# Layer 1's feed-forward block by seven block products in place of eight

## The chip, the cores and the metric

The kernel runs on 1 core of one Trainium2 chip. The metric is device time in microseconds (us), the median of the runs shown. TensorE (PE) does the matmuls, VectorE (DVE) and ScalarE (ACT) elementwise work, GpSimd (POOL) more of it, SyncE (SP) issues all the DMAs.

## What is computed

Two transformer layers over 1024 latent tokens (and 256 context tokens, which only layer 0 carries to its end), model width 1024, FFN width 2816. The change touches only the second layer's SwiGLU block and what leads into it and out of it:

```python
def swiglu(h, w_in, w_out):
    g, u = jnp.split(h @ w_in, 2, axis=-1)
    return (jax.nn.silu(g) * u) @ w_out
...
        x = x + g1 * rms_norm(y, norm_g[l, 1])
        h = rms_norm(x, norm_g[l, 2]) * (1.0 + sc2) + sh2
        x = x + g2 * rms_norm(swiglu(h, ffn_w_in[l], ffn_w_out[l]), norm_g[l, 3])
```

## The kernel before, in words

Activations are held transposed: features on the 128 partitions, tokens along the row. Tokens come in chunks, "a" (0 to 511) and "b" (512 to 1023) in layer 1. A matmul takes a 128x128 weight block and 128x512 activations. Operands are split in two parts, hi and lo (`split`, L396: ACT casts hi, DVE subtracts to get lo), and each product is three matmuls, hi by hi, hi by lo and lo by hi (`mm3`, L404). So 16 weight blocks of a hidden row block (8 for gate, 8 for up) on one chunk are 48 matmuls.

`OutFFN` (L1543) is the output projection and the FFN of one layer. `run` (L1680) first does the projection of chunk a (`p1`) and of b (`p2`), 192 matmuls each. `after` (L1589) follows for each chunk: the residual (`g_residual`, L577), the store of x to DRAM (`X1`), and the second norm (`g_modnorm`, L555), each with a `rstd` (L495: eight one-column matmuls with `ones`, a chain of twelve small POOL instructions) and a `bcast` (L526: four transposes into a bank that DVE then reads). The FFN then goes over NJ = 22 hidden row blocks j. For each j and chunk, `gu` (L1630) does gate and up (48 matmuls) and the activation, and `down` (L1648) multiplies it by the eight 128-column blocks of the down weights (24 matmuls) into eight banks. DVE adds each of those banks to a sum in SBUF. So a j takes 144 matmuls, and the FFN of layer 1 takes 22 x 144 = 3168.

```python
        for f in range(KT):
            ps = pr.b()[:, :n]
...
            pr.mm3(ps, [(wh[:, s], wl[:, s], ah, al)])
            if j == 0:
                pr.nc.scalar.copy(y[f], ps)
            else:
                pr.add(y[f], y[f], ps)
```

The order of the work is not the order of the code. `Recorder` (L48) records every instruction with a cost and its dependencies; `issue` (L160) then plays a list schedule, earliest recorded first among those that are ready and have room in the pools, and emits each engine's instructions in that order. The chip keeps this order on each engine. All instructions therefore carry the line L260 in the profile. Pools: 44 tiles T of 128x1024, 13 tiles U of 128x512, 8 banks b. Names such as T_5897 in the orders below are tiles of those pools.

Of the kernel before, what the change touches and what calls it, by code (L numbers as in the profile page):

```python
# [25 lines left out]
HID = 2816  # L26
NJ = HID // P
# [23 lines left out]
class Recorder:  # L51
# [211 lines left out]
class FM:  # L263
# [7 lines left out]
    def __getitem__(self, kt):  # L271
        o = (kt % self.per) * self.n
        return self.tiles[kt // self.per][:, o:o + self.n]


class Prog:
# [1266 lines left out]
class OutFFN:  # L1543
# [78 lines left out]
    def begin(self):  # L1622
        for k in "gu":
            self.fetch(k, 0)
        for k in "gu":
            self.cv(k, 0)
        for k in "ogu":
            self.fetch(k, k != "o")
# [82 lines left out]
                pr.long(self.finish(c))  # L1711


def program(ctx, nc, tc, d, out):
    nc = Recorder(nc)
    pr = Prog(ctx, nc, tc, d, out)
    pr.setup()
    src0 = {"a": d["xT"][:, 0:512], "b": d["xT"][:, 512:1024], "c": d["ctxT"]}
    h0, h1 = {}, {}
    OT0, OT1 = pr.dram([D, 2, TOK]), pr.dram([D, 2, TOK])  # L1720
    X2 = pr.dram([D, TOK], F32)

# [40 lines left out]
    nc.issue()  # L1763
# [87 lines left out]
```

## Time and profile before

| what | value |
| --- | --- |
| median of 3 runs | 3366.03 us (3363.17 to 3368.88) |
| the profiled execution's own time | 3368.35 us |
| its span, first to last instruction | 3366.3 us |
| PE busy | 3230.5 us (96%) |
| PEld (weight loads) busy | 2677.7 us (80%) |
| DVE, ACT, POOL busy | 2117.3, 1403.2, 617.2 us (63%, 42%, 18%) |
| DMA | 318.20 MB, mean 95 GB/s |

The profiled execution is one more run than the three; it is 2.3 us above their median. Busy shares are averages over stages that have different limits. Layer 1's FFN takes the last fifth of the span, from about 2612 us on.

### The profile page before, as it was taken

How to read it: one execution, taken by the hardware profiler on the slowest of the kernel's cores; microseconds unless marked ns; L12 is line 12 of the kernel's file. 1: busy time of each engine (PE TensorE's matmuls, PEld its weight loads, DVE VectorE, ACT ScalarE, POOL GpSimd, SP SyncE). 2: the span in 40 equal slices, each digit the busy share in tenths (PEclk: the TensorE clock that was granted, in tenths of full speed). 3: DMA queues.
4: the chain of work that ended last, by engine and by line, in shares of the span. 5: the costliest groups of instructions: out<-in, count | busy, mean ns of one | idle time of the engine just before them, and what ended most of it. 6: DMA issues, size and time to landing. Idle time of an engine off the chain costs nothing.

```text
span 3366.3 us, 45397 instructions
## 1 busy us (share of the span) xinstructions
PE 3230.5 (96%) x16916; PEld 2677.7 (80%) x16916; DVE 2117.3 (63%) x4129; ACT 1403.2 (42%) x3208; POOL 617.2 (18%) x943
## 2 busy tenths in 40 slices
PE   7988999999999999999999998999999999999997
PEld 5877778887888888888877896667777788888886
DVE  5569888846444444444478638989985544445445
ACT  3369877854411111111134316778984411111111
POOL 2311100015100000000044716760004200000003
PEclk8999999999999999999999999999999999999998
DMA  6263655344111111111133235432144111111111
GB/s 239 76 221 104 207 160 156 111 161 163 44 38 38 38 38 38 38 38 38 63 115 118 100 117 132 131 110 85 59 170 149 63 57 39 55 51 43 57 57 63
DMA packets 129324, 318.20 MB, mean 95 GB/s; under 512 B 11408, under 2 KB 32592, under 8 KB 129104
## 3 DMA queue, kind: packets, MB, share of 16 engines
q1 hardware_dynamic: 129104, 315.31, 28.8%
q8 instruction: 133, 2.18, 0.3%
q14 instruction: 87, 0.71, 0.1%
HBM read 243.63 MB, written 71.63 MB: 94 GB/s over the span
## 4 chain that ended last, share of the span: by engine, by line
PE 78%; DVE 9%; ACT 4%; POOL 3%; issue 3%; DMA 2%; SPq 0%; POOLq 0%; ACTq 0%; DVEq 0%
PE b L260 78%; DVE T L260 4%; DVE U L260 3%; DVE S L260 3%; ACT T L260 3%; POOL S L260 2%; ACT U L260 2%; POOL U L260 1%; DMA T<-in_ada_w_dram 1%; DMA scr<-T 1%; SPq L260 0%; DMA T<-in_ctxT_dram 0%; POOL T L260 0%; ACT S L260 0%; POOLq L1846 0%
## 5 line engine op out<-in xcount | busy, mean ns | idle before, releaser
L260 PE MATMUL b<-T,T 128*128 128x512 f32 (+5 forms) x9958 | 2172.2, 368 | 33.4 <-ACT T L260 12.8
L260 PEld LDWEIGHTS b<-T,T 128*128 128x128 f32 (+2 forms) x9958 | 1711.7, 190 | 353.4 <-ACT T L260 33.9
L260 PE MATMUL b<-U,T 128*128 128x512 f32 (+2 forms) x3808 | 937.0, 379 | 10.1 <-DVE U L260 3.8
L260 PEld LDWEIGHTS b<-U,T 128*128 128x128 f32 x3808 | 661.4, 189 | 123.0 <-ACT U L260 5.5
L260 DVE TENSOR_TENSOR U<-U,b 128x512 f32<-128x512 f32 (+3 forms) x214 | 134.0, 627 | 619.8 <-PE b L260 607.8
L260 POOL TENSOR_TENSOR U<-U,U 128x512 f32<-128x512 f32 (+1 forms) x130 | 174.9, 1349 | 1696.1 <-ACT U L260 1692.0
L260 DVE TENSOR_TENSOR T<-T,b 128x512 f32<-128x512 f32 (+1 forms) x840 | 482.0, 629 | 0.0
L260 DVE TENSOR_TENSOR T<-T,T 128x1024 fp32r<-128x1024 f32 (+4 forms) x274 | 314.9, 1163 | 232.0 <-PE b L260 173.1
L260 DVE TENSOR_REDUCE S<-b 128x1 f32<-128x512 f32 (+1 forms) x672 | 374.5, 569 | 62.1 <-PE b L260 57.4
L260 ACT ACTIVATE T<-b,S 128x512 f32<-128x512 f32 (+1 forms) x640 | 385.5, 609 | 47.9 <-DVE S L260 42.8
L260 ACT CAST T<-T 128x1024 fp32r<-128x1024 f32 (+3 forms) x202 | 206.1, 1024 | 344.9 <-PE b L260 296.8
L260 DVE TENSOR_TENSOR U<-b,U 128x512 fp32r<-128x512 f32 (+3 forms) x528 | 335.8, 647 | 20.7 <-ACT U L260 16.8
L260 ACT ACTIVATE U<-b 128x256 f32<-128x256 f32 (+1 forms) x148 | 81.3, 552 | 621.6 <-PE b L260 621.3
L260 PE MATMUL b<-ident,T 128*128 128x128 f32 x1968 | 316.7, 277 | 24.6 <-ACT T L260 14.1
L260 ACT CAST U<-b 128x512 fp32r<-128x512 f32 (+3 forms) x528 | 291.1, 565 | 86.1 <-PE b L260 82.6
L260 PEld LDWEIGHTS b<-ident,T 128*128 128x128 f32 x1968 | 238.4, 141 | 89.0 <-ACT T L260 32.0
L260 ACT CAST U<-U 128x512 fp32r<-128x512 f32 (+1 forms) x110 | 63.3, 576 | 305.0 <-DVE U L260 301.0
L260 DVE TENSOR_TENSOR U<-U,U 128x512 fp32r<-128x512 f32 (+4 forms) x167 | 118.9, 712 | 41.1 <-POOL U L260 29.8
L260 ACT ACTIVATE U<-T 128x512 f32<-128x512 f32 (+1 forms) x174 | 96.2, 577 | 96.4 <-DVE T L260 90.3
L260 ACT ACTIVATION_READ_ACCUMULATOR T<-b,S 128x1 f32 x640 | 132.8, 207 | 0.0
L260 ACT CAST T<-U 128x512 fp32r<-128x512 f32 (+3 forms) x122 | 69.4, 572 | 130.9 <-DVE U L260 113.1
L260 POOL TENSOR_TENSOR T<-U,T 128x512 fp32r<-128x512 f32 (+1 forms) x40 | 48.1, 1202 | 386.3 <-ACT T L260 371.3
(71 smaller groups left out, 1519.4 us busy)
## 6 DMA issues: line engine op xcount, KB each, us to landing
scr<-T SPq DMA_DIRECT2D x114, 512.0 KB
T<-in_ada_w_dram SPq DMA_DIRECT2D x96, 512.0 KB
T<-in_ffn_in_dram SPq DMA_DIRECT2D x88, 512.0 KB
T<-scr SPq DMA_DIRECT2D x82, 512.0 KB
T<-scr SPq DMA_DIRECT2D x88, 256.0 KB
T<-in_ffn_out_dram SPq DMA_DIRECT2D x44, 512.0 KB
T<-in_w_out_dram SPq DMA_DIRECT2D x32, 512.0 KB
T<-scr SPq DMA_DIRECT2D x72, 128.0 KB
```

The costliest lines, as they stand in the source:

```text
L260: f(*args, **kw)
```

## The change

Take gate and up of a row block as one product: the weights are a 2x2 block matrix (gate and up by the two halves of the 1024 input features), the activations another (the two feature halves by chunks a and b). Plain multiplication takes eight block products. Winograd's form of Strassen's scheme takes seven, with sums and differences of weight blocks and of activation blocks formed beforehand, and sums of the products afterwards. A block product of gate and up is 4 x 3 = 12 matmuls, so a row block takes 84 in place of 96.

- Activations (`after`): seven sets of four split tiles: B11 and B21 from chunk a alone; B22, T1, T2, T3 and T4 from b and differences of a and b. They occupy 28 of the 44 T tiles.
- `early`: for the first 8 row blocks, the two products that need chunk a alone, with gate of chunk a kept in DRAM (`EA`). `run` does these 8 blocks while b's sets are made.
- `tile`: for each row block the other products (five for the first 8, seven for the other 14), in two banks, with the sums done by accumulation in the bank, by DVE and by POOL. `prep` forms the weight sums on POOL and splits them. The last product (T4) of a row block comes after the next one has begun. The result goes to DRAM (`ACT`).
- `down_all`: after all 22 row blocks, the down projection, also by seven products, for hidden halves and output halves: 7 x 11 steps of 12 matmuls that accumulate in PSUM over 11 row blocks. Each step loads 128x512 weight blocks (nine per t over the seven products) and 128x512 activation blocks (four per t) from DRAM, 256 KB each, forms sums on POOL and DVE, and splits both operands.

Matmuls: 22 x 84 + 77 x 12 = 2772 in place of 3168. The diff, cut to its core:

```diff
+class WinoFFN(OutFFN):
+    EARLY = 8
+    HALF = NJ // 2
...
+    def put_set(self, name, k, x):
+        pr = self.pr
+        t = pr.T(F32R)
+        hi, lo = t[:, 0:512], t[:, 512:1024]
+        pr.split(x, hi, lo)
+        self.sets.setdefault(name, {})[k] = (hi, lo)
+        if len(self.sets[name]) == 4:
+            self.ready.add(name)
+    def after(self, c):
...
+        if c == "a":
+            for kt in range(KT):
+                norm(kt)
+                self.put_set("B11" if kt < 4 else "B21", kt % 4, y[kt])
+                if kt % 2:
+                    yield 3.0
+            return
+        a = self.hf["a"]
+        for k in range(4):
+            norm(k)
+            norm(k + 4)
+            self.put_set("B22", k, y[k + 4])
+            pr.sub(a[k], y[k], a[k])
+            yield 2.6
+            self.put_set("T1", k, a[k])
+            pr.tt(y[k], y[k + 4], y[k], ALU.subtract, eng=nc.gpsimd)
+            pr.sub(a[k], y[k + 4], a[k])
+            self.put_set("T2", k, a[k])
+            yield 2.4
+            pr.tt(a[k + 4], a[k + 4], a[k], ALU.subtract, eng=nc.gpsimd)
+            self.put_set("T3", k, y[k])
+            self.put_set("T4", k, a[k + 4])
+            yield 2.4
+        self.hf.clear()
+    def prod(self, ps, name, w, o, first):
+        pr = self.pr
+        (wh, oh), (wl, ol) = w
+        x = self.sets[name]
+        for k in range(4):
+            hi, lo = x[k]
+            h, q = wh[:, oh + o + k * P:oh + o + k * P + P], wl[:, ol + o + k * P:ol + o + k * P + P]
+            pr.mm(ps, h, hi, first and k == 0, False)
+            pr.mm(ps, h, lo, False, False)
+            pr.mm(ps, q, hi, False, k == 3)
+        pr.tick(2.7)
+    def early(self, j):
+        pr, nc = self.pr, self.pr.nc
+        if j + 2 < self.EARLY:
+            self.fetch("g", j + 2)
+        if j + 1 < self.EARLY:
+            self.gsplit(j + 1)
+        w = self.conv.pop(("g", j))
+        x, z = pr.b(), pr.b()
+        e = pr.T()
+        self.prod(x, "B11", w, 0, True)
+        nc.scalar.copy(e[:, 0:512], x)
+        pr.until(lambda: "B21" in self.ready)
+        self.prod(z, "B21", w, 512, True)
+        pr.add(e[:, 512:1024], e[:, 0:512], z)
+        nc.scalar.activation(e[:, 512:1024], e[:, 512:1024], AF.Silu)
+        pr.load(self.EA[j * P:(j + 1) * P, :], e)
+    def prep(self, j):
...
+        g, u = self.raws.pop(("g", j)), self.raws.pop(("u", j))
+        gp = nc.gpsimd
+        s = pr.T()
+        pr.tt(s[:, 0:512], u[:, 0:512], u[:, 512:1024], ALU.add, eng=gp)
+        pr.tt(s[:, 512:1024], s[:, 0:512], g[:, 0:512], ALU.subtract, eng=gp)
+        hi, lo = pr.wsplit(s)
+        self.conv["s12", j] = ((hi, 0), (lo, 0))
+        pr.tt(u[:, 0:512], g[:, 0:512], u[:, 0:512], ALU.subtract, eng=gp)
+        t = pr.T(F32R)
+        pr.split(u[:, 512:1024], t[:, 0:512], t[:, 512:1024])
+        self.conv["u", j] = ((t, 0), (t, 512))
+        pr.tt(u[:, 512:1024], g[:, 512:1024], s[:, 512:1024], ALU.subtract, eng=gp)
+        hi, lo = pr.wsplit(u)
+        self.conv["s34", j] = ((hi, 0), (lo, 0))
+    def tile(self, j):
+        pr, nc = self.pr, self.pr.nc
+        late = j < self.EARLY
+        x, y = pr.b(), None
+        s12, s34, u = (self.conv.pop((k, j)) for k in ("s12", "s34", "u"))
+        act = pr.T()
+        if late:
+            e = self.raws.pop(("e", j))
+            s1, sa = e[:, 0:512], e[:, 512:1024]
+            self.last()
+        else:
+            g = self.conv.pop(("g", j))
+            s1, sa = pr.U(), pr.U()
+            self.prod(x, "B11", g, 0, True)
+            nc.scalar.copy(s1, x)
+            self.last()
+            z = pr.b()
+            self.prod(z, "B21", g, 512, True)
+            pr.add(sa, s1, z)
+            nc.scalar.activation(sa, sa, AF.Silu)
+        self.raw(j + 2)
+        y = pr.b()
+        self.prod(y, "T1", s12, 0, True)
+        s5 = pr.U()
+        nc.scalar.copy(s5, y)
+        self.prod(x, "T2", s12, 512, late)
+        sb = pr.U()
+        if late:
+            pr.add(sb, s1, x)
+            pr.tt(s5, s5, s1, ALU.add, eng=nc.gpsimd)
+        else:
+            nc.scalar.copy(sb, x)
+        self.prep(j + 1)
+        self.prod(y, "B22", s34, 512, False)
+        pr.add(sb, sb, y)
+        nc.scalar.activation(sb, sb, AF.Silu)
+        self.prod(x, "T3", s34, 0, False)
+        pr.add(s5, s5, x)
+        pr.mul(act[:, 512:1024], sb, s5)
+        def last():
+            self.prod(x, "T4", u, 0, False)
+            if late:
+                pr.add(s5, s1, x)
+                pr.mul(act[:, 0:512], sa, s5)
+            else:
+                pr.mul(act[:, 0:512], sa, x)
+            pr.later(lambda: pr.load(self.ACT[j * P:(j + 1) * P, :], act))
+            self.last = lambda: None
+        self.last = last
+    PRODS = ("P1", "P5", "P6", "P3", "P7", "P2", "P4")
+    def dload(self, k):
...
+        for a in {"P1": [(0, 0)], "P5": [(0, 1)], "P6": [(1, 1)], "P2": [(1, 0)]}.get(p, []):
+            act(*a)
+        for b in {"P1": [(0, 0)], "P5": [(1, 0), (1, 1)], "P6": [(0, 0)], "P3": [(0, 1)], "P7": [(0, 0), (1, 0)],
+                  "P2": [(0, 1)], "P4": [(1, 1)]}[p]:
+            w(*b)
+    def dprep(self, k):
...
+        if p == "P5":
+            if t % 2 == 0:
+                self.sw[t // 2] = pr.T()
+        s = self.sw[t // 2][:, (t % 2) * 512:(t % 2) * 512 + 512] if p in ("P5", "P6", "P3") else raw[0]
+        if p == "P1":
+            x = k1[:, lo]
+        elif p == "P5":
+            x = k1[:, lo]
+            pr.sub(x, k1[:, hi], x)
+            pr.tt(s, raw[0], raw[1], ALU.add, eng=gp)
+        elif p == "P6":
+            x = k1[:, lo]
+            pr.sub(x, k2[:, hi], x)
+            pr.tt(s, s, raw[0], ALU.subtract, eng=gp)
+        elif p == "P3":
+            x = k2[:, hi]
+            pr.tt(s, raw[0], s, ALU.subtract, eng=gp)
+        elif p == "P7":
+            x = k1[:, hi]
+            pr.sub(x, k2[:, hi], x)
+            pr.tt(s, raw[0], raw[1], ALU.subtract, eng=gp)
+        elif p == "P2":
+            x = k2[:, lo]
+        else:
+            x = k1[:, lo]
+            pr.sub(x, k2[:, lo], x)
+        ws, xs = pr.T(F32R), pr.T(F32R)
+        pr.split(s, ws[:, lo], ws[:, hi])
+        pr.split(x, xs[:, lo], xs[:, hi])
+        self.dop[k] = (ws, xs)
+    def down_all(self):
...
+        LOADS, PREPS = 4, 2
+        for k in range(LOADS):
+            self.dload(k)
+        for k in range(PREPS):
+            self.dprep(k)
+        for k in range(7 * H):
+            p, t = self.PRODS[k // H], k % H
+            self.dload(k + LOADS)
+            self.dprep(k + PREPS)
+            ws, xs = self.dop.pop(k)
+            kind = "x" if p in ("P1", "P6", "P7", "P4") else "y"
+            new = t == 0 and p in ("P1", "P5", "P2")
+            if new:
+                bank[kind] = [pr.b() for _ in range(4)]
+            for f in range(4):
+                wh, wl = (ws[:, o + f * P:o + f * P + P] for o in (0, 512))
+                ps = bank[kind][f]
+                pr.mm(ps, wh, xs[:, 0:512], new, False)
+                pr.mm(ps, wh, xs[:, 512:1024], False, False)
+                pr.mm(ps, wl, xs[:, 0:512], False, t == H - 1)
+            pr.tick(2.7)
...
+    def run(self, hook=None):
+        pr, first, rest = self.pr, self.first, self.rest
+        pr.drain_slow()
+        self.p1.run((len(first) * KT - 2, self.p2.start))
+        self.p2.run((KT - 3, self.begin))
+        pr.until(lambda: "B11" in self.ready)
+        for j in range(self.EARLY):
+            self.early(j)
+        self.raw(0)
+        self.raw(1)
+        self.prep(0)
+        pr.until(lambda: len(self.ready) == 7)
+        for j in range(NJ):
+            self.tile(j)
+        self.last()
+        while pr.bg:
+            pr.tick(0)
+        self.sets.clear()
+        self.down_all()
...
-    f1 = OutFFN(pr, 1, "ab", OT1, lambda c: X2[:, CHUNKS[c][0]:CHUNKS[c][0] + CHUNKS[c][1]], put3, None)
+    f1 = WinoFFN(pr, 1, "ab", OT1, lambda c: X2[:, CHUNKS[c][0]:CHUNKS[c][0] + CHUNKS[c][1]], put3, None)
```

The order of the two programs is the same, up to tile numbers, on PE, DVE, ACT and POOL until the end of layer 1's output projection. After it, three places matter.

DVE from the first instruction after chunk b's second `bcast` (the bank b_5901 before, b_5895 in the change). Before, it scales y into U (bank as a source) and subtracts hi:

```order
L260 SCALAR_TENSOR_TENSOR U_5910<-T_5785,der_80,b_5901 128x512
L260 SCALAR_TENSOR_TENSOR U_5911<-T_5785,der_80,b_5901 128x512
L260 SCALAR_TENSOR_TENSOR U_5912<-T_5786,der_80,b_5901 128x512
L260 SCALAR_TENSOR_TENSOR T_5906<-U_5910,mod_78,T_5902 128x512
L260 SCALAR_TENSOR_TENSOR T_5906<-U_5911,mod_78,T_5902 128x512
```

And in the change, where T_5896 is part of B22, T_5897 of T1, T_5899 of T3:

```order
L260 SCALAR_TENSOR_TENSOR T_5787<-T_5787,der_80,b_5895 128x512
L260 SCALAR_TENSOR_TENSOR T_5789<-T_5789,der_80,b_5895 128x512
L260 SCALAR_TENSOR_TENSOR T_5787<-T_5787,der_80,b_5895 128x512
L260 TENSOR_TENSOR T_5737<-T_5787,T_5737 128x512
L260 SCALAR_TENSOR_TENSOR T_5789<-T_5789,der_80,b_5895 128x512
L260 TENSOR_TENSOR T_5737<-T_5787,T_5737 128x512
L260 TENSOR_TENSOR T_5896<-T_5789,T_5896 128x512
L260 TENSOR_TENSOR T_5897<-T_5737,T_5897 128x512
L260 TENSOR_TENSOR T_5899<-T_5787,T_5899 128x512
```

Up to the split of the first row block's weight sums (T_5944 below) this goes on for 39 DVE instructions: 8 with a scalar and the bank, 3 additions from a bank, 27 with two SBUF sources of 128x512 and one of 128x1024. Beside them stand 11 POOL additions of 128x512, and from the transposes to the last early product 72 matmuls on PE.

PE at the end of the early products (bank b_5930) in the change, the first row block's T1 product in b_5953 and T2 in b_5948. T_5943 and T_5944 are the hi and lo of its weight sums:

```order
L260 MATMUL b_5930<-T_5835,T_5921 128x512 x2
L260 MATMUL b_5930<-T_5835,T_5922 128x512
L260 MATMUL b_5953<-T_5897,T_5943 128x512 x2
L260 MATMUL b_5948<-T_5898,T_5943 128x512 x2
L260 MATMUL b_5953<-T_5897,T_5944 128x512
L260 MATMUL b_5953<-T_5908,T_5943 128x512 x2
```

Before, the same place has the gate product of chunk b, as soon as each part of its activations (T_5902) is there:

```order
L260 MATMUL b_5901<-ident,S_5898 128x128 x4
L260 MATMUL b_5930<-U_5888,T_5868 128x512
L260 MATMUL b_5933<-T_5902,T_5844 128x512
L260 MATMUL b_5934<-T_5902,T_5846 128x512
L260 MATMUL b_5942<-T_5902,T_5870 128x512
```

Four matmuls of the first row block stand ahead of the one that needs T_5944; all others stand behind it.

DVE in the down projection. Before, between two row blocks, it adds banks to the sums in SBUF:

```order
L260 TENSOR_TENSOR U_6193<-U_6193,b_6192 128x512
L260 TENSOR_TENSOR T_5947<-T_5947,b_6196 128x512
L260 TENSOR_TENSOR T_5947<-T_5947,b_6197 128x512
L260 TENSOR_TENSOR U_6195<-U_6193,U_6194 128x512
L260 TENSOR_TENSOR T_5948<-T_5948,b_6198 128x512
```

In the change, at the start of the second product (P5), it makes the operands of the third (P6) and differences for the fifth (P7):

```order
L260 TENSOR_TENSOR T_6410<-T_6354,T_6410 128x512
L260 TENSOR_TENSOR T_6411<-T_6300,T_6411 128x512
L260 TENSOR_TENSOR T_6300<-T_6399,T_6300 128x512
L260 TENSOR_TENSOR T_6414<-T_6354,T_6414 128x512
L260 TENSOR_TENSOR T_6304<-T_6408,T_6304 128x512 x2
L260 TENSOR_TENSOR T_6415<-T_6302,T_6415 128x512
```

None of these has a bank as a source. From the first weight sum on POOL (T_6354) to the last operand of P6 stand 92 DVE instructions (89 of them with two SBUF sources), 42 POOL additions and, up to P6's last step, 400 matmuls.

## Rows read from the trace of the kernel before

**Rows 1.** Cores: span and mean granted clock.

```profile
core 0: 3366.3 us, clock 0.986
```

**Rows 2.** The page's chain of waits that ended last, shares by engine.

```profile
PE 78%; DVE 9%; ACT 4%; POOL 3%; issue 3%; DMA 2%; SPq 0%; POOLq 0%; ACTq 0%; DVEq 0%
```

**Rows 3.** Windows: stretch, length, busy us and count per engine, clock, DMA share, GB/s.

```profile
2750.00:2850.00 100.00, 100.00 (x443) 82.84 (x442) 48.81 (x71) 16.82 (x22) 0.00 (x0) 1.00 0.14 48
```

**Rows 4.** Timeline of SP in the FFN: start, length, transfer, count.

```profile
2696.56 1.41 SPq L260 DMA_DIRECT2D T<-in_ffn_in_dram  x2
...
2729.20 1.40 SPq L260 DMA_DIRECT2D T<-in_ffn_in_dram  x2
...
2761.84 1.40 SPq L260 DMA_DIRECT2D T<-in_ffn_in_dram  x2
```

**Rows 5.** Timeline of PE at the FFN's start, with idle before and releaser.

```profile
2596.61 19.56 PE L260 MATMUL b<-T,T 128*128 128x512 f32 x85
2616.01 0.94 PE L260 MATMUL b<-ones,U 128*128 128x1 f32 x8
2616.82 4.39 PE L260 MATMUL b<-T,T 128*128 128x512 f32 x18
2621.04 0.60 PE L260 MATMUL b<-ident,S 128*128 128x128 f32 x4
2621.39 13.89 PE L260 MATMUL b<-T,T 128*128 128x512 f32 x60
2636.56 1.42 PE L260 MATMUL b<-U,T 128*128 128x512 f32 x5 [1.27 <-ACT U L260]
2638.27 1.05 PE L260 MATMUL b<-ones,U 128*128 128x1 f32 x8 [0.29 <-POOL U L260]
2639.95 4.42 PE L260 MATMUL b<-U,T 128*128 128x512 f32 x18 [0.63 <-DVE U L260]
2644.64 0.65 PE L260 MATMUL b<-ident,S 128*128 128x128 f32 x4 [0.28 <-POOL S L260]
2645.05 0.48 PE L260 MATMUL b<-U,T 128*128 128x512 f32 x1
2646.96 22.37 PE L260 MATMUL b<-T,T 128*128 128x512 f32 x96 [1.43 <-ACT T L260]
```

**Rows 6.** Timeline of DVE, four places where POOL is idle.

```profile
2591.67 1.21 DVE L260 TENSOR_TENSOR T<-T,T 128x1024 fp32r<-128x1024 f32 x1
...
2623.00 1.29 DVE L260 TENSOR_TENSOR T<-T,T 128x512 f32<-128x512 f32 x2
...
2645.40 2.06 DVE L260 SCALAR_TENSOR_TENSOR U<-T,der,b 128x512 f32<-128x512 f32 x3 [3.40 <-PE b L260]
...
2704.58 3.67 DVE L260 TENSOR_TENSOR T<-T,b 128x512 f32<-128x512 f32 x6
```

**Rows 7.** Timelines of DVE and POOL: POOL by itself, then both at once.

```profile
2625.03 1.29 POOL L260 TENSOR_TENSOR U<-U,U 128x512 f32<-128x512 f32 x1 [4.30 <-ACT U L260]
...
2579.33 11.26 DVE L260 TENSOR_TENSOR T<-T,T 128x512 f32<-128x512 f32 x6
...
2574.53 17.20 POOL L260 TENSOR_TENSOR U<-U,U 128x512 f32<-128x512 f32 x9 [1.42 <-ACT U L260]
```

**Rows 8.** Windows ahead of the FFN, columns as in rows 3.

```profile
2580.00:2590.00 10.00, 5.90 (x29) 4.62 (x27) 10.00 (x6) 5.73 (x8) 9.84 (x6) 1.00 0.77 275
2590.00:2600.00 10.00, 10.00 (x43) 8.24 (x43) 5.83 (x9) 3.48 (x6) 6.31 (x14) 0.83 0.45 162
...
2585.00:2590.00 5.00, 0.90 (x7) 0.48 (x5) 5.00 (x3) 1.57 (x2) 4.92 (x4) 1.00 1.03 393
```

**Rows 9.** Timelines of PE and of SP at the end of the program.

```profile
3330.71 11.04 PE L260 MATMUL b<-U,T 128*128 128x512 f32 x48
...
3316.99 45.86 SPq L260 DMA_DIRECT2D out_dram<-T  x8
```

More of the change, by code (lines that the diff above doesn't have):

```diff
@@ L1711, in run, with __init__, norm, begin @@
                 pr.long(self.finish(c))
+class WinoFFN(OutFFN):
+    EARLY = 8
+    HALF = NJ // 2
+    def __init__(self, *args):
+        super().__init__(*args)
+        self.hf, self.sets, self.ready = {}, {}, set()
+        self.ACT = self.pr.dram([HID, 1024], F32)
+        self.EA = self.pr.dram([self.EARLY * P, 1024], F32)
+    def put_set(self, name, k, x):
[7 more added lines that the diff above has]
+    def after(self, c):
+        pr, l, nc = self.pr, self.l, self.pr.nc
+        n = CHUNKS[c][1]
+        y = self.y.pop(c)
+        acc2 = pr.accs()
+        yield from pr.g_residual(y, self.acc.pop(c), self.xsrc(c), pr.vec(pr.der[l], 1, c), acc2)
+        dst = self.view(self.X1, c)
+        for i, t in enumerate(y.tiles):
+            pr.load(dst[2 * i * P:2 * i * P + 2 * P, :].rearrange("(k p) n -> p k n", p=P),
+                    t.rearrange("p (k n) -> p k n", n=n))
+        cols = pr.rstd(acc2, n, D)
+        yield -RSW
+        rb = pr.bcast(cols)
+        A, Bv = pr.vec(pr.der[l], 2, c), pr.mvec(l, 3, c)
+        def norm(kt):
+            pr.stt(y[kt], y[kt], A(kt), rb[:, :n])
+            nc.scalar.activation(y[kt], y[kt], AF.Identity, bias=Bv(kt))
+        self.hf[c] = y
+        if c == "a":
[33 more added lines that the diff above has]
+        pr.tick(2.7)
+    def begin(self):
+        for j in range(2):
+            self.fetch("g", j)
+        self.gsplit(0)
+    def gsplit(self, j):
+        hi, lo = self.pr.wsplit(self.raws.pop(("g", j)))
+        self.conv["g", j] = ((hi, 0), (lo, 0))
+    def early(self, j):
[14 more added lines that the diff above has]
+        pr.load(self.EA[j * P:(j + 1) * P, :], e)
+    def raw(self, j):
+        if j < NJ:
+            for kind in "gu":
+                self.fetch(kind, j)
+            if j < self.EARLY:
+                e = self.raws["e", j] = self.pr.T()
+                self.pr.load(e, self.EA[j * P:(j + 1) * P, :])
+    def prep(self, j):
+        if j >= NJ:
+            return
+        pr, nc = self.pr, self.pr.nc
+        if j >= self.EARLY:
+            g = self.raws["g", j]
+            hi, lo = pr.wsplit(g)
+            self.conv["g", j] = ((hi, 0), (lo, 0))
+        g, u = self.raws.pop(("g", j)), self.raws.pop(("u", j))
[13 more added lines that the diff above has]
+    def tile(self, j):
+        pr, nc = self.pr, self.pr.nc
+        late = j < self.EARLY
[45 more added lines that the diff above has]
+        self.last = last
+    def last(self):
+        pass
+    PRODS = ("P1", "P5", "P6", "P3", "P7", "P2", "P4")
+    def dload(self, k):
+        if k >= 7 * self.HALF:
+            return
+        pr, H = self.pr, self.HALF
+        p, t = self.PRODS[k // H], k % H
+        def act(half, c):
+            j = t + half * H
+            if j not in self.at:
+                self.at[j] = pr.T()
+            pr.load(self.at[j][:, c * 512:(c + 1) * 512], self.ACT[j * P:(j + 1) * P, c * 512:(c + 1) * 512])
+        def w(r, s):
+            raw = pr.U()
+            j = t + s * H
+            pr.load(raw, pr.d["ffn_out"][self.l, j * P:(j + 1) * P, r * 512:(r + 1) * 512])
+            self.wr.setdefault(k, []).append(raw)
+        for a in {"P1": [(0, 0)], "P5": [(0, 1)], "P6": [(1, 1)], "P2": [(1, 0)]}.get(p, []):
[4 more added lines that the diff above has]
+    def dprep(self, k):
+        if k >= 7 * self.HALF:
+            return
+        pr, H = self.pr, self.HALF
+        gp = pr.nc.gpsimd
+        p, t = self.PRODS[k // H], k % H
+        raw = self.wr.pop(k)
+        k1, k2 = self.at.get(t), self.at.get(t + H)
+        lo, hi = slice(0, 512), slice(512, 1024)
+        if p == "P5":
[28 more added lines that the diff above has]
+        self.dop[k] = (ws, xs)
+        if p == "P4":
+            self.at.pop(t)
+            self.at.pop(t + H)
+    def down_all(self):
+        pr, nc, H = self.pr, self.pr.nc, self.HALF
+        self.at, self.wr, self.sw, self.dop = {}, {}, {}, {}
+        ya, yb = FMs(pr), FMs(pr)
+        self.yacc = {"a": ya, "b": yb}
+        bank = {}
+        LOADS, PREPS = 4, 2
[4 more added lines that the diff above has]
+        for k in range(7 * H):
+            p, t = self.PRODS[k // H], k % H
+            self.dload(k + LOADS)
[12 more added lines that the diff above has]
+            pr.tick(2.7)
+            if t < H - 1:
+                continue
+            if p == "P7":
+                self.acc["b"] = pr.accs(1 if self.next_norm else 2)
+            if p == "P4":
+                self.acc["a"] = pr.accs(1 if self.next_norm else 2)
+            for f in range(4):
+                ps = bank[kind][f]
+                if p == "P1":
+                    nc.scalar.copy(ya[f], ps)
+                elif p == "P5":
+                    nc.scalar.copy(yb[f + 4], ps)
+                elif p == "P6":
+                    nc.scalar.copy(yb[f], ps)
+                elif p == "P3":
+                    pr.add(yb[f], yb[f], ps)
+                elif p == "P7":
+                    pr.add(yb[f + 4], yb[f + 4], ps)
+                    pr.sq_add(self.acc["b"], yb[f], 512, 2 * f)
+                    pr.sq_add(self.acc["b"], yb[f + 4], 512, 2 * f + 1)
+                elif p == "P2":
+                    pr.add(ya[f], ya[f], ps)
+                else:
+                    nc.scalar.copy(ya[f + 4], ps)
+                    pr.sq_add(self.acc["a"], ya[f], 512, 2 * f)
+                    pr.sq_add(self.acc["a"], ya[f + 4], 512, 2 * f + 1)
+            if p == "P7":
+                pr.long(self.finish("b"))
+        pr.long(self.finish("a"))
+    def run(self, hook=None):
[17 more added lines that the diff above has]
+        self.down_all()
@@ L1714, in program, with __init__, __getitem__, tiles @@
+class FMs:
+    def __init__(self, pr):
+        self.pr, self.n, self.per, self.t = pr, 512, 2, {}
+    def __getitem__(self, kt):
+        i = kt // 2
+        if i not in self.t:
+            self.t[i] = self.pr.T()
+        return self.t[i][:, (kt % 2) * 512:(kt % 2) * 512 + 512]
+    @property
+    def tiles(self):
+        return [self.t[i] for i in range(4)]
 def program(ctx, nc, tc, d, out):
```

## The prediction

> **What bounds the kernel now.** I read first the cores: 3366.3 us at a mean clock of 0.986 [rows 1], so the throttle has little to give back. The chain of waits gives PE 78% and DVE 9% [rows 2]. A share is a mean over stages, so I went to the stage that changes. In a stretch of 100 us of layer 1's FFN, PE is busy for all 100.00 us at clock 1.00, DVE for 48.81, ACT for 16.82, POOL for nothing, and the DMAs take a share of 0.14 [rows 3]. That stage is bound by PE alone: a matmul fewer is time gained, at the price that PE pays there. SP issues each row block's loads every 32.64 us (2696.56, 2729.20, 2761.84) [rows 4]; a row block is 144 matmuls, so one costs 0.2267 us. Some matmul records are missing from a trace, so this is better than dividing by a count of records.
>
> The other engines matter once work is put on them. DVE alone takes 0.60 us from one 128x512 operation with two SBUF sources to the next (two in 1.29 us, the last one's tail included), 0.66 for one with a scalar and a bank, 0.61 for an addition from a bank, 1.21 for 128x1024 [rows 6]. A POOL addition alone takes 1.29 us. Where both engines had such work, DVE took 11.26 us for six (1.88 each) and POOL 17.20 us for nine (1.91 each) [rows 7]. 0.60 + 1.29 is 1.89: they took turns, and each waited out the other's whole instruction. So I add up the two engines' times wherever both are queued on two SBUF sources.
>
> **The change part by part.** The sum is made against the profiled execution, 3368.35 us by its own time, which is 2.3 above the median of 3366.03.
>
> *Matmuls.* 3168 - 2772 = 396 fewer, at 0.2267: **-89.8**.
>
> *Entry.* The old start of the FFN had five idle gaps on PE, 1.27 + 0.29 + 0.63 + 0.28 + 1.43 = 3.9 us, while chunk b's norm was made [rows 5]: -3.9. The norm's chain (squares on ACT, rstd on POOL, transposes, bcast) stays, and only PE's early products lie beside it. I step PE to the second `ones` at about 2636.0; POOL delivers at 2638.3, where the old `ones` began [rows 5], so PE waits 2.3, and about 1.3 more for the bcast: +3.6.
>
> Then the sets. Before, PE went on after 1.43 us, because the gate product takes chunk b's activations one by one. Now the first row block needs its weight sums' split T_5944, behind 39 DVE instructions: 8 x 0.66 + 3 x 0.61 + 27 x 0.60 + 1.21 = 24.5 us if POOL is out of the way [rows 6]. Eleven POOL additions stand beside them, 14.2 us alone [rows 7]. By strict turns that is 38.7; if POOL runs freely under the 11 instructions that read a bank (7.1 us, room for three), eight additions count, 8 x 1.29 = 10.3, and I get about **35**. That is my choice. No row shows a bank reader beside POOL. The Trainium skill, "SBUF — State Buffer", section "Who interferes with whom", says that only a DVE instruction with two SBUF inputs meets GpSimd's reads; by that the 35 holds, without it 38.7. DVE begins at 2645.40 [rows 6], so T_5944 is there at 2680.4. PE has 72 matmuls from the transposes at 2644.64 [rows 5], 16.3 us and 0.4 for the transposes, then four that do not need T_5944, 0.9: it stands at 2662.3. The wait is **+18** (24.5 gives 7.6, 38.7 gives 22). After a wait the clock is lower: behind a stretch of 5 us in which PE was busy for 0.90, the next 10 us ran at a granted 0.83, between 1.2 and 2.4 GHz [rows 8]; 0.17 x 10 is +1.7. Entry in all: -3.9 + 3.6 + 18 + 1.7 = **+19.4**.
>
> *Row blocks.* Eight late ones of 60 matmuls (13.6 us) and fourteen of 84 (19.0 us). I add DVE and POOL of a late one in turns to about 10 us of the 13.6 and take them as covered. What is left is banks that PE must accumulate into again as soon as DVE has read them: 0.25 us for each late block (nothing, to a whole bank addition of 0.61 [rows 6]) and 0.5 at the first block's second weight sums: +2.5, between 0 and 5. A late block moves about 2 MB (gate and up weights, EA, ACT), 154 GB/s where 393 has been seen [rows 8]: 0. At the last row block no next one covers T4: three two-source operations, one POOL addition in turn and one bank addition are 1.8 + 1.29 + 0.61 = 3.7 us, less the 7 matmuls between, 1.6: **+2.1**.
>
> *Down.* From P5's first weight sum to P6's last operand: 89 x 0.60 + 3 x 0.61 + 42 x 1.29 = 109.4 us in turns [rows 6, 7], against 400 x 0.2267 = 90.7 of PE and about 2.5 of work made ahead, 93.2. The bounds are 0 (the engines overlap after all) and 16.2. I take 12, nearer the upper end, since the only stretch in which both were queued shows turns, and some waiting for ACT's casts beside which POOL is free: **+12**, spread over P6. P6's operands are tiles that P5 frees, so DVE cannot run further ahead. P3, P7, P2 and P4 ask for less and cost 0 (P7 again has one sum on each engine per step, but its differences are made during P5). The 22 x 8 bank additions per chunk that DVE did are gone, which frees DVE and not PE: 0.
>
> *End.* The last matmul ends at 3341.75 and the program 24.5 us later, after the last norm and eight stores [rows 9]. The order after the last product is of the same kind: +0.3 for one more bank copy.
>
> **Sum:** -89.8 + 19.4 + 2.5 + 2.1 + 12 + 0.3 = -53.5. On the profiled execution 3314.9, on the median 3312.6: **3313**.
>
> **The rivals.**
> *R1, it is nearly all hidden.* DVE and POOL overlap better than rows 7 show, so the entry's wait is 7.6 and P6 does not stall: -89.8 + 9.0 + 2.1 + 2.0 = -76.7, **3289**. For it: one stretch alone shows turns, and a sum is less late if POOL is ahead. Against: that stretch is exact, 1.88 and 1.91 for 1.89.
>
> *R2, DVE and POOL set the pace for longer.* The entry is at its upper bound (+23.4), the late blocks at theirs (+4.9), P6 at 16.2, and each of the fourteen full blocks waits for one POOL addition more, 14 x 1.29 = 18.1: -89.8 + 23.4 + 4.9 + 2.1 + 16.2 + 18.1 = -25.1, **3341**. For it: POOL, idle before [rows 3], forms every weight sum. Against: a full block gives 19 us for much the same sums as a late one's 13.6.
>
> *R3, slower: the down phase waits for its transfers.* It loads 99 weight and 44 activation blocks of 256 KB, 143 in all, over 924 matmuls, 209.5 us. If they went one after another at the price of a lone store, 512 KB in 3.4 us (issued by 3362.85, program ended at 3366.3 [rows 9]), that is 486 us: 277 more than PE's, -53.5 + 277, about **3590**. It decides for slower from (209.5 + 53.5) / 143 = 1.84 us per transfer. Against: with several queued, the trace moves 393 GB/s [rows 8], 256 KB in 0.67 us; P5, the hungriest product, asks for three in 2.72 us, 289 GB/s, and loads stand four steps ahead, 10.9 us. The Trainium skill, "DMA: Bandwidth & Descriptors", section "Anatomy of one DMA", speaks against this change: for its GpSimd path it fits a fixed 2.0 us per DMA plus bytes over 436 GB/s, an estimate of 2.6 us for 256 KB. Taken per transfer with no overlap, it makes the kernel slower; the 393 GB/s of this trace contradicts that.
>
> **How the numbers follow.** The main case, in which DVE and POOL take turns in the two places named, gets 0.75; its own range, from the bounds of the entry (7.6 to 22) and of P6 (0 to 16), is 3295 to 3325. R1 gets 0.12, R2 0.10, R3 0.03. The range takes in R1 with a little for the end, 3286, and reaches to R2, 3342; what is left out is R3 and the outer halves of R1 and R2. About 0.2% (6.7 us) is what a measurement of this kernel can tell from no change. All cases but R3 are faster by more: faster 0.96, same 0.01, slower 0.03.
>
> **What would show it right or wrong.** Right: full row blocks 19.04 us apart and late ones 13.6; one wait of PE of some 18 us near 2662, ended by DVE, with POOL and DVE at 1.9 us per instruction before it, and a granted clock under 1 behind it; short waits of PE for DVE in P6, 12 us together; DMAs under 300 GB/s in P5 and no wait for them. Wrong: waits of PE for a DMA in the down phase (R3); gaps at each full row block (R2); an entry wait under 10 (R1); or a wait at a place not named here, such as a bank that DVE frees late.

## The result, and the profile after

The change takes 3304.37 us (median of 4 runs, 3301.75 to 3307.14) against 3364.60 (3362.24 to 3368.88, 4 runs): a ratio of 0.982, 95% interval 0.9803 to 0.9837, 60.2 us less. Forecast were 3313, a range of 3286 to 3342, and 53.5 less.

The profiled execution of the change has a span of 3300.0 us. That of before has 3366.3 [rows 1], 66.3 more. Not all of this is the change: the `ones` matmuls of chunk a's second norm, ahead of which both programs have the same order, begin at 2616.01 before [rows 5] and at 2611.52 after. 4.5 us are a difference between two executions; **61.8** come behind that place, and this is what the terms below have to give.

The page of the change, its chain of waits that ended last, shares by engine:

```profile
PE 75%; DVE 11%; ACT 4%; POOL 3%; issue 3%; DMA 3%; SPq 0%; POOLq 0%; ACTq 0%; DVEq 0%
```

PE is still the engine that bounds; DVE has a little more of the chain than in [rows 2]. The timeline of PE from the FFN's start to the last product answers to [rows 5] (start, length, count, and in brackets the idle time before with what ended it):

```profile
2611.52 0.95 PE L260 MATMUL b<-ones,U 128*128 128x1 f32 x8
...
2616.91 15.03 PE L260 MATMUL b<-T,T 128*128 128x512 f32 x65
2635.81 1.05 PE L260 MATMUL b<-ones,U 128*128 128x1 f32 x8 [3.88 <-POOL U L260]
2636.73 6.20 PE L260 MATMUL b<-T,T 128*128 128x512 f32 x19
...
2643.12 16.61 PE L260 MATMUL b<-T,T 128*128 128x512 f32 x72
2667.88 2.08 PE L260 MATMUL b<-T,T 128*128 128x512 f32 x4 [8.15 <-ACT T L260]
2677.15 7.18 PE L260 MATMUL b<-T,T 128*128 128x512 f32 x22 [7.20 <-DVE T L260]
2684.71 7.32 PE L260 MATMUL b<-T,T 128*128 128x512 f32 x31 [0.38 <-DVE T L260]
2692.87 361.73 PE L260 MATMUL b<-T,T 128*128 128x512 f32 x1594 [0.84 <-DVE U L260]
3055.65 83.30 PE L260 MATMUL b<-T,T 128*128 128x512 f32 x366 [1.04 <-DVE U L260]
3140.61 3.06 PE L260 MATMUL b<-T,T 128*128 128x512 f32 x12 [1.66 <-DVE T L260]
3145.81 3.06 PE L260 MATMUL b<-T,T 128*128 128x512 f32 x12 [2.15 <-DVE T L260]
3149.80 3.03 PE L260 MATMUL b<-T,T 128*128 128x512 f32 x12 [0.94 <-DVE T L260]
3153.79 88.94 PE L260 MATMUL b<-T,T 128*128 128x512 f32 x391 [0.96 <-DVE T L260]
```

Read it from the top. The chain of the second norm (ended by POOL) costs 3.88 us. Then come 72 early matmuls and the hole that the forecast put at 18 us, in two pieces: 8.15 us until ACT has cast the first row block's weight sums to hi (T_5943), four matmuls, and 7.20 us until DVE has made their lo part (T_5944). The forecast had one wait, ended by DVE. From 2692.87 on PE runs without a gap for 361.73 us, up to the last row block's T4, which waits 1.04. In P6 and at the start of P3 there are four waits for DVE, 1.66 + 2.15 + 0.94 + 0.96 = 5.71 us. Nothing waits for a DMA.

What the clock did in the hole, in the windows of the change (columns as in [rows 3]; the third from the end is the granted clock):

```profile
2660.00:2670.00 10.00, 2.08 (x4) 1.16 (x4) 10.00 (x13) 7.41 (x12) 6.29 (x4) 0.71 0.13 52
2670.00:2680.00 10.00, 2.85 (x7) 2.27 (x8) 8.30 (x12) 4.58 (x8) 4.78 (x4) 0.50 0.63 206
2680.00:2690.00 10.00, 9.62 (x40) 7.55 (x39) 5.44 (x5) 3.33 (x5) 8.60 (x6) 0.94 0.32 108
```

PE was busy for 2.08 of 10 us, and for the next 10 us the granted clock was 0.50, the lower of its two levels (1.2 GHz of 2.4). So the four matmuls between the two waits took 2.08 us, and the 22 behind them 7.18. What that cost is read from rows at either level: 65 matmuls at full speed take 15.03, that is 65 x 0.2267 and 0.3 for the last one's tail. By the same measure 19 matmuls in 6.20 lost 1.6 us, 4 in 2.08 lost 0.9, 22 in 7.18 lost 1.9: 4.4 in all.

The timeline of SP, two late row blocks apart (first two rows), then one full one:

```profile
2712.80 3.25 SPq L260 DMA_DIRECT2D T<-in_ffn_in_dram  x2
...
2740.04 3.25 SPq L260 DMA_DIRECT2D T<-in_ffn_in_dram  x2
...
2855.51 1.81 SPq L260 DMA_DIRECT2D T<-in_ffn_in_dram  x2
...
2874.55 1.81 SPq L260 DMA_DIRECT2D T<-in_ffn_in_dram  x2
```

27.24 us for two late row blocks, 13.62 each for 60 matmuls, and 19.04 for a full one of 84: the same 0.2267 us a matmul as in [rows 4].

DVE and POOL, first at the entry. DVE's timeline in the change:

```profile
2643.64 2.06 DVE L260 SCALAR_TENSOR_TENSOR T<-T,der,b 128x512 f32<-128x512 f32 x3
...
2646.88 12.50 DVE L260 TENSOR_TENSOR T<-T,T 128x512 f32<-128x512 f32 x12
...
2661.82 0.67 DVE L260 TENSOR_TENSOR T<-T,b 128x512 f32<-128x512 f32 x1
2662.42 0.73 DVE L260 SCALAR_TENSOR_TENSOR T<-T,der,b 128x512 f32<-128x512 f32 x1
2663.08 3.75 DVE L260 TENSOR_TENSOR T<-T,T 128x512 fp32r<-128x512 f32 x4
...
2674.81 3.49 DVE L260 TENSOR_TENSOR T<-T,T 128x512 fp32r<-128x512 f32 x4
```

and POOL's beside it:

```profile
2662.13 2.95 POOL L260 TENSOR_TENSOR T<-T,T 128x512 f32<-128x512 f32 x2 [3.30 <-ACT T L260]
```

The burst begins at 2643.64, and PE is released at 2677.15: 33.5 us, forecast 35. Twelve two-source operations took 12.50 us where 7.3 would do alone. At 2662.13 POOL begins two additions; DVE's instruction that then reads a bank takes its usual 0.73, and the two-source ones behind it are stretched. The forecast says that no row shows a bank reader beside POOL. The trace of before does show it, inside POOL's run from 2574.53 to 2591.73 [rows 7], where two such take no longer than by themselves [rows 6]:

```profile
2578.01 1.39 DVE L260 SCALAR_TENSOR_TENSOR T<-T,der,b 128x512 f32<-128x512 f32 x2
```

The Trainium skill, "SBUF — State Buffer", section "Who interferes with whom", says that a DVE instruction with at most one SBUF input, outside the 2-port modes, does not contend with GpSimd, and that one with two does when GpSimd reads SBUF. The trace agrees: 0.73 and 1.39 us are the times of DVE alone, and the stretched instructions have two SBUF sources.

Then the down projection: DVE and POOL side by side in P5, DVE's timeline in P6, and P5's window (POOL's busy time stands before the clock, the DMA share and GB/s behind it):

```profile
3074.54 1.77 DVE L260 TENSOR_TENSOR T<-T 128x512 f32<-128x512 f32 x1
3076.24 1.78 DVE L260 TENSOR_TENSOR T<-T,T 128x512 fp32r<-128x512 f32 x1
...
3074.03 11.94 POOL L260 TENSOR_TENSOR T<-T,U 128x512 f32<-128x512 f32 x7
```

```profile
3094.45 63.64 DVE L260 TENSOR_TENSOR T<-T,T 128x512 f32<-128x512 f32 x63
```

```profile
3064.00:3094.00 30.00, 30.00 (x134) 24.86 (x133) 30.00 (x24) 9.74 (x17) 25.42 (x15) 1.00 0.92 313
```

DVE is busy for all of it. At one DVE instruction to one POOL addition, in the first rows, both go on every 1.70 us: the addition costs DVE 1.70 - 0.60 = 1.10 us. In the 63.64 us of P6 stand 63 DVE instructions and 23 POOL additions by POOL's timeline, nearly three to one: (63.64 - 63 x 0.60) / 23 = 1.12. So the price is 1.1 at either mix, and not POOL's whole 1.29, which the forecast took from [rows 7]; the part on why the prediction was right says how. The DMAs moved 313 GB/s at a share of 0.92, over the 300 that the forecast named, and PE waited for none of them.

### The profile page after: what moved, and what is told of

Same layout as the page of the kernel before. It is cut to its first block, busy times and chain, and to the rows that moved or that the text cites. A ratio compares the mean times of both kernels' runs of the same rounds, so it can differ in the third digit from the quotient of the medians.

```text
span 3300.0 us, 45509 instructions
## 1 busy us (share of the span) xinstructions
PE 3147.5 (95%) x16520; PEld 2605.2 (79%) x16520; DVE 2156.7 (65%) x4083; ACT 1525.0 (46%) x3426; POOL 841.1 (25%) x1091
## 4 chain that ended last, share of the span: by engine, by line
PE 75%; DVE 11%; ACT 4%; POOL 3%; issue 3%; DMA 3%; SPq 0%; POOLq 0%; ACTq 0%; DVEq 0%
PE b L260 75%; DVE T L260 6%; DVE U L260 3%; DVE S L260 3%; ACT T L260 2%; ACT U L260 2%; POOL U L260 2%; POOL S L260 1%; DMA T<-in_ada_w_dram 1%; DMA scr<-T 1%; DMA U<-scr 0%; DMA U<-in_ffn_out_dram 0%; DMA T<-scr 0%; POOL T L260 0%; DMA T<-in_ctxT_dram 0%
## 5 line engine op out<-in xcount | busy, mean ns | idle before, releaser
L260 PE MATMUL b<-T,T 128*128 128x512 f32 (+5 forms) x10618 | 2321.4, 370 | 55.2 <-DVE T L260 22.1
L260 PEld LDWEIGHTS b<-T,T 128*128 128x128 f32 (+2 forms) x10618 | 1837.5, 190 | 404.8 <-ACT T L260 41.3
L260 PE MATMUL b<-U,T 128*128 128x512 f32 (+2 forms) x2752 | 692.3, 376 | 7.3 <-DVE U L260 3.2
L260 DVE TENSOR_TENSOR T<-T,T 128x1024 fp32r<-128x1024 f32 (+4 forms) x475 | 499.7, 1078 | 218.8 <-PE b L260 111.3
L260 PEld LDWEIGHTS b<-U,T 128*128 128x128 f32 x2752 | 465.2, 191 | 78.9 <-issue 5.0
L260 ACT CAST T<-T 128x1024 fp32r<-128x1024 f32 (+3 forms) x362 | 300.7, 845 | 359.4 <-PE b L260 245.4
L260 DVE TENSOR_TENSOR T<-T,b 128x512 f32<-128x512 f32 (+1 forms) x524 | 283.1, 594 | 17.1 <-PE b L260 17.1
L260 POOL TENSOR_TENSOR T<-T,T 128x512 f32<-128x512 f32 x146 | 203.3, 1403 | 118.5 <-DVE T L260 104.9
L260 ACT COPY U<-b 128x512 f32<-128x512 f32 (+3 forms) x175 | 96.2, 550 | 171.9 <-PE b L260 170.2
L260 POOL TENSOR_TENSOR T<-U,T 128x512 fp32r<-128x512 f32 (+2 forms) x51 | 66.4, 1302 | 404.6 <-ACT T L260 371.2
```

What stands on the lines that cost most here:

```text
L260: f(*args, **kw)
```

## The experiments

Four questions: is the hole at the entry the burst on DVE and nothing else (e1, e5, e6); does POOL hold DVE up, at the entry (e3) and in P6 (e2); is the down projection otherwise bound by PE (e4); and do the repairs add (e7). The runs of before that stand beside e1 to e4 have a median of 3368.42, those beside e5 to e7 3366.94; so differences under 4 us are read from the traces.

**e1, three early blocks more.**

```diff
-    EARLY = 8
+    EARLY = 11
```

> Eleven early row blocks in place of eight: 72 more matmuls (16.3 us) lie on PE beside the making of chunk b's sets. Theory A (PE waits at the first full-scheme row block only because DVE and POOL, taking turns, need 33.5 us for the sets and the first weight sums): the two waits there, 8.15 + 7.20 us, shrink to 3 us or less together, the low clock behind them (about 4 us) goes too, and the kernel takes 3285 to 3290 us, 15 to 19 less than the change. Rival B (DVE and POOL set the pace for longer, so that the wait only moves into the late row blocks, now eleven of them): PE waits in the late blocks add up to over 8 us, and the time is 3297 or more.

3295.85 us, ratio 0.9786 (0.9771 to 0.9801): between the two. Its timeline of PE:

```profile
2647.20 17.52 PE L260 MATMUL b<-T,T 128*128 128x512 f32 x76
2667.21 1.27 PE L260 MATMUL b<-T,T 128*128 128x512 f32 x4 [2.49 <-ACT T L260]
2668.68 2.08 PE L260 MATMUL b<-T,T 128*128 128x512 f32 x4 [0.20 <-ACT T L260]
2672.53 29.14 PE L260 MATMUL b<-T,T 128*128 128x512 f32 x115 [1.77 <-DVE T L260]
2702.96 346.00 PE L260 MATMUL b<-T,T 128*128 128x512 f32 x1524 [1.30 <-DVE U L260]
```

The hole at the first row block is gone, but PE now waits among the early products. By the program's order, the matmuls behind these waits need the hi parts (ACT) and a lo part (DVE) of the early blocks' own weights, whose splits stand among the sets in both queues. The clock stayed low as well: 115 matmuls in 29.14 lost 2.8 us. The waits fell by 10.8 us, and from the common `ones` (2615.59 here) to the end it takes 9.9 less. More cover brings work of its own to the engines that are late. Neither theory had this.

**e2, the down projection's weight sums on DVE** (four lines, all alike):

```diff
-            pr.tt(s, raw[0], raw[1], ALU.add, eng=gp)
+            pr.tt(s, raw[0], raw[1], ALU.add)
```

> The down projection's weight sums on DVE in place of POOL. Theory A (turns: each POOL addition holds DVE for its whole 1.29 us): DVE's own work from P5's first sum to P6's last operand is 131 x 0.60 + 1.8 = 80 us, less than PE's 93, so the four waits in P6 (1.66 + 2.15 + 0.94 + 0.96 = 5.7 us) and their low clock (1 us) go: 3297 to 3299 us. Rival B (POOL works freely beside DVE, and DVE alone is late): 42 additions more on DVE, 25 us, and P6's waits grow to 10 us or more. Rival C (P6's operands are late for tiles or loads): the waits stay near 5.7.

3293.92 us, ratio 0.9776 (0.9759 to 0.9792): 3 us below A's range. The timeline of PE has one row from the first row block to the end norm, and the window of P5 shows POOL idle:

```profile
2695.41 541.54 PE L260 MATMUL b<-T,T 128*128 128x512 f32 x2387 [0.84 <-DVE U L260]
```

```profile
3064.00:3094.00 30.00, 30.00 (x134) 24.82 (x134) 28.06 (x47) 12.89 (x22) 0.00 (x0) 1.00 0.95 338
```

All four waits of P6 are gone, and T4's 1.04. DVE did 47 instructions in 30 us where it had done 24 beside POOL, and was no longer full. Theory A holds in its cause: giving DVE more work made DVE faster, because a POOL addition had cost DVE 1.1 us and costs 0.60 on DVE itself. From the common `ones` (2613.96 here) to the end it takes 9.1 us less than the change. These waits are 6.75. The same 2387 matmuls are busy for 543.1 us in the change's six rows and for 541.54 here, so each of the five waits costs some 0.3 more than its idle time, the tail of the last matmul ahead of it: 1.6. And in the end norm, after the same wait, 14 matmuls with `ones` ran faster (rows of the change, e2 and e4):

```profile
3279.07 3.15 PE L260 MATMUL b<-ones,U 128*128 128x1 f32 x14 [3.06 <-DVE U L260]
3273.28 2.28 PE L260 MATMUL b<-ones,U 128*128 128x1 f32 x14 [3.06 <-DVE U L260]
3299.90 1.72 PE L260 MATMUL b<-ones,U 128*128 128x1 f32 x14 [3.06 <-DVE U L260]
```

That is 0.9, and the sum 9.2.

**e3, the gate and up part's sums on DVE** (the sets, the weight sums of `prep`, the addition to s5):

```diff
-            pr.tt(y[k], y[k + 4], y[k], ALU.subtract, eng=nc.gpsimd)
+            pr.tt(y[k], y[k + 4], y[k], ALU.subtract)
...
-        pr.tt(s[:, 0:512], u[:, 0:512], u[:, 512:1024], ALU.add, eng=gp)
+        pr.tt(s[:, 0:512], u[:, 0:512], u[:, 512:1024], ALU.add)
```

> In the gate and up part (sets, weight sums, the late blocks' addition) all that POOL added is on DVE; the down projection keeps POOL. Theory A (turns): from DVE's first instruction after the second bcast to the first row block's lo weight sums 24.5 + 11 x 0.60 = 31 us in place of 33.5, so the two waits are 2 to 3 us shorter together; row blocks stay bound by PE: 3300 to 3303. Rival B (POOL's additions were free beside DVE): that stretch grows by 6.6 us, to 40, and the time with it, to 3311.

3302.36 us, ratio 0.9805 (0.979 to 0.9819), no different from the change within the runs. The hole is one wait of 16.18 us, where the change has 8.15 + 7.20 + 0.38 + 0.84 = 16.57. DVE's row at its end closes with the lo weight sums:

```profile
2680.73 377.09 PE L260 MATMUL b<-T,T 128*128 128x512 f32 x1651 [16.18 <-ACT T L260]
...
2678.25 3.68 DVE L260 TENSOR_TENSOR T<-T,T 128x512 fp32r<-128x512 f32 x5
```

By A's own measure, from DVE's first instruction (2648.46) to the lo weight sums (2681.93), it is 33.5 us, as in the change and not 31. Two things cancel. DVE now does 53 instructions in that time, three more than the 50 that A counted, where the change has 39. The 14 more are about 8.4 us at 0.60, and POOL's eleven additions had cost DVE 33.5 - 24.5 = 9.0. Besides, the weight sums, which POOL had made beside the sets, now stand behind all of them on DVE, and the cast waits for them. So POOL's additions were not free, and B, 6.6 us more, is out; but A's gain at PE did not come.

**e4, the down projection by eight plain block products** (each output block summed in its banks over 22 steps, no sums of operands):

```diff
+        steps = [(c, r, s, t) for c in "ba" for r in (0, 1) for s in (0, 1) for t in range(H)]
...
+            first, end = s == 0 and t == 0, s == 1 and t == H - 1
...
-                pr.mm(ps, wh, xs[:, 0:512], new, False)
+                pr.mm(ps, wh, xs[:, 0:512], first, False)
```

> Gate and up as in the change, the down projection by eight plain block products accumulated in PSUM (1056 matmuls in place of 924), no weight or activation sums in it. Theory A (the down phase is bound by PE, at 0.2267 us a matmul, but for the waits in P6): +29.9 for 132 matmuls, -6.7 for P6's waits and their clock, 3327 us. Rival B (the seven products save little because DVE, POOL or the loads set the pace there): 3315 or less.

3323.42 us, ratio 0.9867 (0.9852 to 0.9882), 19 more than the change; from the common `ones` on, 20.0 more by the two traces. Its timeline has no wait of PE from the first row block to the end norm. 132 matmuls less T4's and P6's waits would be 29.9 - 6.75 = 23.2. The 3 us between are the two small terms of e2: 1.6 for the tails at five waits, and 3.15 - 1.72 = 1.4 at the end norm's `ones`. A holds and B is out: leaving out the eighth product saves what PE pays for it, less the waits that the sums bring.

**e5, early weights split three blocks ahead**, with eleven early blocks:

```diff
-        if j + 2 < self.EARLY:
-            self.fetch("g", j + 2)
-        if j + 1 < self.EARLY:
-            self.gsplit(j + 1)
+        for i in ([*range(2, 5)] if j == 0 else [j + 4]):
+            if i < self.EARLY:
+                self.fetch("g", i)
+        for i in ([*range(1, 4)] if j == 0 else [j + 3]):
+            if i < self.EARLY:
+                self.gsplit(i)
```

> Eleven early row blocks as in the first run, and the early blocks' own weights split three blocks ahead in place of one, so that most of those splits lie ahead of chunk b's sets on ACT and DVE. Theory A (in the first run PE waited 2.49 + 0.20 + 1.77 us for the early blocks' own splits, queued among the sets, and not for the sets): these waits and most of the low clock (some 4 us) go, and the time is 3287 to 3291 us, 5 to 8 less than the first run. Rival B (DVE has so much to do up to the first full-scheme block that a wait only moves from the early blocks to that block): PE's waits between the second transposes and the second row block stay at 4 us or more in sum, and the time at 3294 or more.

3288.32 us, ratio 0.9763 (0.9749 to 0.9778): A. Its timeline of PE:

```profile
2637.25 1.05 PE L260 MATMUL b<-ones,U 128*128 128x1 f32 x8 [2.07 <-POOL U L260]
2638.17 4.33 PE L260 MATMUL b<-T,T 128*128 128x512 f32 x18
...
2670.84 5.29 PE L260 MATMUL b<-T,T 128*128 128x512 f32 x22 [0.20 <-DVE T L260]
2679.08 1.20 PE L260 MATMUL b<-T,T 128*128 128x512 f32 x4 [2.96 <-ACT T L260]
2680.76 359.41 PE L260 MATMUL b<-T,T 128*128 128x512 f32 x1575 [0.49 <-DVE T L260]
```

The waits at the early blocks are gone, as A says; 0.20 + 2.96 + 0.49 = 3.65 us are left of the change's 16.57, a little under the 4 that B named, and the clock is full through the early products (122 in 27.95 us). Behind the 2.96 it is not: 1575 matmuls in 359.41 lost 2.0. And not all of the gain is A's: of the 8.1 us that it takes less than e1 from the common `ones` on, 3.7 lie ahead of the second transposes, where the norm's wait is 2.07 in place of 3.88 and the matmuls behind it run at full speed. Why that wait is shorter was not tried.

**e6, one set after another, T1 first**, and the first weight sums two early blocks sooner, with eight early blocks:

```diff
         for k in range(4):
             norm(k)
-            norm(k + 4)
-            self.put_set("B22", k, y[k + 4])
             pr.sub(a[k], y[k], a[k])
-            yield 2.6
             self.put_set("T1", k, a[k])
+            if k % 2:
+                yield 3.6
+        for k in range(4):
+            norm(k + 4)
...
+            if j == 6:
+                self.raw(0)
+                self.prep(0)
```

> Eight early blocks as in the change; the sets are made one after another (all four tiles of T1, then T2, then B22, T3 and T4) in place of four tiles wide, and the first row block's weight sums are recorded two early blocks sooner. No work is added or removed. Theory A (the wait of 15.4 us is for the end of the whole burst on DVE, since T1's last tile and the weight sums are at its end): the first block's products begin while the other sets are still being made, so that the two waits fall to 8 us or less in sum, and with the low clock the time falls by 7 to 10 us, to 3294 to 3297. Rival B (the total of DVE and POOL work up to the second row block counts, whatever its order): the waits only spread over the first block's products, their sum stays at 13 us or more, and the time within 3 us of the change's.

3300.62 us, ratio 0.9802 (0.9786 to 0.9819). Its timeline:

```profile
2642.78 12.61 PE L260 MATMUL b<-T,T 128*128 128x512 f32 x53
2661.98 2.07 PE L260 MATMUL b<-T,T 128*128 128x512 f32 x4 [6.59 <-ACT T L260]
2670.93 380.74 PE L260 MATMUL b<-T,T 128*128 128x512 f32 x1667 [6.88 <-DVE T L260]
```

6.59 + 6.88 = 13.47, so B by its bound of 13, though the time is 3.8 us less than the change's, a little more than B's 3. But the edit did not change the order of the sets alone. Only 53 early matmuls stand ahead of the first wait, where the change has 72, and after the second wait ACT still copies a bank of an early block, released by PE:

```profile
2677.76 0.59 ACT L260 COPY T<-b 128x512 f32<-128x512 f32 x1 [1.11 <-PE b L260]
```

By the code the split of the last early block's weights is now recorded behind the first row block's weight sums, so PE had less cover when the wait began. Whether the order of the sets matters by itself is therefore not shown. What helped much was work taken ahead of the burst (e5) or off the shared turns (e2).

**e7, e5 and e2 together.**

> The fifth run's early blocks and the second run's weight sums of the down projection on DVE, together. If the two waits are independent (one at the entry, one in P6), the gains add: the fifth run's time less 8 us for P6's and the last T4's waits, some 3280 us. If DVE's free time was shared between them, less than 4 us is gained over the fifth run.

3279.05 us (3277.49 to 3280.48), ratio 0.9736 (0.9721 to 0.975): the gains add, and this version beats both kernels. PE's waits in its timeline are 2.07 before the second norm's `ones`, 0.19 + 2.92 + 0.49 at the entry, and none in P5 to P4.

## Why the prediction was right, and where it was off

The direction, the place of the largest wait and its cause were right; the gain was 60.2 where 53.5 was forecast, and the difference is in the sizes of terms, one of which rests on a misread row. From the profiled executions:

- *Matmuls, -89.8.* Full blocks are 19.04 us apart, late ones 13.6 on average, as worked out. e4 pays 20.0 for 132 more, in agreement with that once its waits, tails and end norm are counted.
- *Entry, +19.4.* Measured: 3.88 + 8.15 + 7.20 + 0.38 + 0.84 = 20.45 of idle, less 3.9 of the old gaps, and 4.4 of low clock: +21.0. The hole was 15.35 where 18 was forecast; the norm's wait 3.88 where 2.3 + 1.3 was, all of it ahead of `ones` and none for the bcast. The four matmuls that the forecast let run ahead of the hole needed T_5943 and waited for ACT, a wait that it put at nothing; since T_5944 ended the hole, this moved part of the wait and added little. On DVE the eleven POOL additions cost 9.0 us, where the forecast counted 10.3 for eight. Its "room for three" under the bank readers has no working (7.1 us hold five at 1.29), so that 35 came so near 33.5 is in part luck. The clock's term was sized by one stretch with a wait of 4 us (1.7); two waits so close that the clock did not rise in between cost 4.4.
- *Row blocks, +2.5.* The 0.38 and 0.84 of the first block are counted above; behind them no late block waited. *T4 of the last block, +2.1*: 1.04, with its tail 1.3.
- *Down, +12.* This is the term that was furthest off: "nearer the upper end" of 0 to 16.2. It was 5.71, with the four tails 6.9. The cause, turns on DVE and POOL, is shown by e2. The price of 1.29 per POOL addition was misread. A row of the timeline prints the shape of its first instruction, and the six of [rows 7] are not alike; a narrower window shows that the last four are twice as wide, with 1.21 us each alone [rows 6]:

```profile
2581.64 8.95 DVE L260 TENSOR_TENSOR T<-T,T 128x1024 fp32r<-128x1024 f32 x4
```

They go on every 2.2 us, 1.1 more than alone. So the price there is 1.1 too, and the agreement of 1.88 and 1.91 with 0.60 + 1.29, which the forecast calls exact and holds against R1, was chance. The stretch that it put at 109.4 us has the 92 DVE instructions and 42 POOL additions that it counted, and ran from 3049.72 to 3149.74, just before PE's last step of P6 begins: 100.0 us. Less the forecast's 93.2 for PE that is 6.8. Inside it PE waited for T4 and for the first three waits of P6, 1.04 + 1.66 + 2.15 + 0.94 and four tails: 7.0.
- *End, +0.3.* From the last product to the end: 24.1 us (3275.9 to 3300.0), 24.5 before [rows 9]: -0.4.

Sum: -89.8 + 21.0 + 1.3 + 6.9 - 0.4 = -61.0, against the 61.8 of the spans.

Two sums of the forecast do not follow. By its own bounds the main case spans 3290 to 3321, not 3295 to 3325. And R3's 486 us charge each 256 KB with the 3.4 us of a store of 512 KB; by bytes it is 1.7 each, 243 in all, and R3 would not have made the kernel slower.

R1 took the entry's wait at 7.6 and none in P6; 15.35 and 5.71 were measured, and e2 shows that POOL's additions are what P6 waited for. R2's waits at each full block do not exist. R3 is out: P5 moved 313 GB/s, e2 338, and no wait of PE in the down projection was ended by a DMA; the per-transfer sum that the forecast made from the Trainium skill, "DMA: Bandwidth & Descriptors", section "Anatomy of one DMA", is no measure of transfers that are queued four steps ahead.

## What to carry to other kernels

A scheme that saves matmuls pays on the engines that form its sums. Price them in turns where two of them read SBUF, from instructions of one known shape, and look for the one place where everything must be there at once: here the entry, not the long loop. A price that fits a sum to the last digit can still come from a row that mixes shapes. Sums on a slower engine were no help while they held up a faster one; moving them to the faster one, and moving unrelated work ahead of the burst, gained 25 us more.

## What was not expected of the hardware

- A POOL addition of 128x512 takes 1.29 us by itself and costs DVE 1.1: at one to one (1.70 us a pair in P5), at three to one (1.12 in P6), and beside DVE operations of 128x1024 (2.2 in place of 1.1). Why it is less than 1.29 was not tried.
- After a wait of 2.07 us (e5, the `ones` at 2637.25) the next 18 matmuls ran at full speed, 4.33 us; after 3.88 us (the change) 19 took 6.20. Between two waits of 8.15 and 7.20 the clock stayed at 0.50 although PE worked. After the same wait of 3.06 at the end norm, 14 matmuls took 3.15, 2.28 and 1.72 us in three kernels.
- DMA shares of 0.92 and 0.95, 313 and 338 GB/s, and no wait for them.
